# First loads in another order with zeros multiplied meanwhile, VectorE in written order around the latents' norm, and the gates' running sum moved behind six attention steps

## The chip, the cores and the metric

The kernel runs on one core of a Trainium2 chip. The metric is the device time of one execution in microseconds (us); lower is better. Everything below is about the start of a program whose profiled span is 3190.3 us, and about the same place in its second layer. "TensorE" is the engine of the matrix products (PE in the profile; its weight loads are PEld), "VectorE" is DVE, "ScalarE" is ACT, "GpSimd" is POOL, "SyncE" is SP, and the last one only issues loads and stores here.

## The reference

Two blocks of two layers each run one behind the other on 512 tokens of width 1024, all in fp32. The change touches the first block alone. Each of its layers begins with one product of the tokens with a wide weight matrix, whose columns are cut into the inputs of four kinds of attention:

```python
def first_block(x, w_in, fox_b_f, mla_g_q, mla_g_kv, mla_w_uq, mla_w_ukv, swa_sinks, mix_g, w_o, ...):
    for l in range(DEPTH):
        h = x @ w_in[l]
        (fq, fk, fv, fgate, cq, ckv, kr, sq, sk, sv, wq, wk, wv) = jnp.split(h, points, axis=-1)
        log_f = jax.nn.log_sigmoid(fgate + fox_b_f[l])
        cum = jnp.cumsum(log_f, axis=1).transpose(0, 2, 1)
        out_a = _causal_softmax_blocks(_heads(fq, FOX_H), _heads(fk, FOX_H), _heads(fv, FOX_H),
                                       HEAD_DIM ** -0.5, cum)
        out_b = _mla(cq, ckv, kr, mla_g_q[l], mla_g_kv[l], mla_w_uq[l], mla_w_ukv[l], cos, sin)
        out_c = _stick_breaking_blocks(_heads(sq, SB_H), _heads(sk, SB_H), _heads(sv, SB_H))
        out_d = _swa_sink_alibi(_heads(wq, SWA_H), _heads(wk, SWA_KV_H), _heads(wv, SWA_KV_H),
                                swa_sinks[l], slopes)
        ...  # mix, output product, layer norm, feed-forward network, layer norm

def _mla(cq, ckv, kr, g_q, g_kv, w_uq, w_ukv, cos, sin):
    q = (_rmsnorm(cq, g_q) @ w_uq).reshape(B, S, MLA_H, MLA_NOPE + MLA_ROPE)
    kv = (_rmsnorm(ckv, g_kv) @ w_ukv).reshape(B, S, MLA_H, MLA_NOPE + MLA_V)
    ...
```

Three pieces matter here. The *latents* are `cq` (256 columns), `ckv` (128) and the rope key `kr` (32); `cq` and `ckv` are normed and then multiplied with `mla_w_uq` and `mla_w_ukv`. The four columns `fgate` are the gates, whose running sum of logarithms `cum` enters the scores of `out_a` alone (called fox in the kernel). `wq`, `wk` and `wv` feed `out_d`.

## The kernel before

**Products.** An fp32 product is made of three products of high and low parts: high weight by high x, high weight by low x, low weight by high x (`mm3`, lines 157 to 161; the last of the three is line 160). The high part is a cast on ScalarE, the low part a subtraction on VectorE. For x these tiles are XH and XL, for weights `whi` and `wlo`. `wchunk` (line 138) loads a chunk of weights into one of three `raw` buffers from SyncE's queue; unless the caller does it himself (`split=False`), it makes `whi` (line 145) and `wlo` (line 148), of which there are four buffers each. A later load into a raw buffer waits until the cast and the subtractions that read it are done.

**What sets the order.** TensorE's instructions stand in the order in which the code is written. On the other engines a scheduler puts the instructions in order by its own costs, except inside a `tc.manual_schedule` of that engine: there too the written order holds. At the start of the first layer this is so for VectorE and ScalarE, up to `order.close()`. An engine takes its instructions strictly in the order of the program that comes out, so an instruction that waits holds up all that stand behind it. `later(t, f)` puts the products of f into TensorE's order after t us of further products, by the code's own cost of a product.

**The start of a layer.** In layer 0, x arrives in four blocks of 128 tokens (`load_x`), and `turn_x` transposes two blocks at a time on TensorE (tile xT); ScalarE copies the result to XH, VectorE makes XL, and ScalarE copies it once more to X. In layer 1 XH and XL come out of the layer norm before. Then comes *hg*: the product of the 420 columns 768 to 1188 of `w_in` (gates, cq, ckv, kr), loaded as two chunks of four row blocks with 260 columns and two with 160, with some of the columns written twice in another order. `half_units` makes hg for one half of the tokens after the other, 96 products of 256 columns each; in layer 0 the transposes of the second half of x stand among those of the first. ScalarE copies the latents out to `lat`, VectorE the rope key and the gates to `mz` (line 738).

Behind hg stand, in written order: `tables` (rope, masks, sel and alibi tables, loaded from GpSimd's queue and cast on VectorE), `lat_norm` (sum of squares `s`, and by `later` their sums on TensorE, the inverse root in 12 small VectorE instructions, its broadcast on TensorE, and the high and low parts LH and LL of the normed latents), `forget` (the rotated key `rope`, and the gates' running sum: Identity, Abs, Exp and Ln on ScalarE, a scan on VectorE, written to CR), `g_mla_w` (the weights `mla_w_uq` and `mla_w_ukv` are loaded and split into `uhl` and `kvhl`), and two *units* of 512 tokens by 256 weight columns each (`g_unit` at column 1956 for wq, at 2212 for wk and wv; tile u). A unit takes two chunks of four row blocks, so 16 steps of three products of 512 columns. The call `flush()` puts what `later` still holds ahead of the rest. The products that use LH and LL (`drain(gw)`) come after the first unit and half of the second.

**The attention steps.** Then 64 steps run in a pipeline with a lag of three (`run_steps`): scores into one of two PSUM banks (sc), exponential on ScalarE (PR), transpose (pt, copied to PT), product with the values (pv). The pauses are filled with the products of further units. Steps 0 to 15 are `_mla`, 16 to 31 `out_d`, 32 to 47 stick breaking, and 48 to 63 fox, the only ones that read CR.

## Time and profile before

| what | value |
|---|---|
| runs | 3192.87, 3191.55, 3190.7 us (median 3191.55 us) |
| profiled execution | 3192.1 us, of which its span is 3190.3 us |
| mean granted TensorE clock | 0.998 |
| busy, TensorE | 3150.4 us (99% of the span) |
| busy, VectorE | 1611.0 us (50%) |
| busy, ScalarE | 1164.5 us (37%) |
| busy, GpSimd | 128.3 us (4%) |
| moved by DMA | 289.95 MB, mean 91 GB/s |

The span is the time between the first and the last instruction of the profiled execution; its own time has 1.8 us more around it. A busy TensorE is not one at its peak: when the granted clock is at half, its products take longer and it counts as busy all the same.

### The profile page before, as it was taken

Reading aid. Unit: us, or ns where it says so; the run is one execution under the profiler, and the core shown is the slowest. Engines: PE = TensorE matmul, PEld = TensorE weight load, DVE = VectorE, ACT = ScalarE, POOL = GpSimd, SP = SyncE. Lnnn points to the kernel's source line nnn. Section 1 sums busy time; section 2 is a strip of 40 time slices with the busy share of each in tenths; the row PEclk is TensorE's granted clock in tenths of the full one; section 3 lists DMA queues with packets and bytes.
Section 4 is the critical chain, followed back from the end, with each engine's and each line's share of the span. In section 5 each row is a group of like instructions: output and inputs, shape, how many; then the busy total and the mean of one; then the engine's idle time right before and its main releaser. Section 6 shows DMA issues by size and latency. Waiting matters only on the chain.

```text
span 3190.3 us, 40511 instructions
## 1 busy us (share of the span) xinstructions
PE 3150.4 (99%) x16376; PEld 2657.1 (83%) x16376; DVE 1611.0 (50%) x2804; ACT 1164.5 (37%) x1945; POOL 128.3 (4%) x176
## 2 busy tenths in 40 slices
PE   8999999999999999999999999999999999999999
PEld 7878888997788888988888788888888888788888
DVE  6566333475664334844336764433444336754433
ACT  5454322264533222533224443322323224443322
POOL 1002000020020000000001000000000000000000
PEclk9999999999999999999999999999999999999999
DMA  4111333341113333333333223333333333133322
GB/s 140 47 40 54 111 99 96 109 133 40 54 54 100 99 96 116 114 95 99 95 97 95 81 80 93 99 96 96 95 103 93 96 106 89 57 95 101 96 95 84
DMA packets 285355, 289.95 MB, mean 91 GB/s; under 512 B 10260, under 2 KB 282208, under 8 KB 285168
## 3 DMA queue, kind: packets, MB, share of 16 engines
q1 hardware_dynamic: 281792, 281.15, 29.4%
q0 software_dynamic: 2944, 5.17, 0.6%
q8 instruction: 128, 2.10, 0.3%
q10 hardware_dynamic: 432, 1.05, 0.1%
q14 instruction: 59, 0.48, 0.0%
HBM read 285.22 MB, written 2.11 MB: 90 GB/s over the span
## 4 chain that ended last, share of the span: by engine, by line
PE 94%; DVE 4%; ACT 1%; issue 1%; DMA 0%; DVEq 0%; SPq 0%; ACTq 0%
PE u L158 17%; PE u L160 17%; PE u L159 17%; PE o L159 7%; PE o L158 7%; PE o L160 7%; PE pv L638 2%; PE oh L158 2%; PE oh L159 2%; PE oh L160 2%; PE pt L631 1%; PE hg L158 1%; PE hg L159 1%; PE hg L160 1%; PE sc L951 1%; PE ut L520 1%
## 5 line engine op out<-in xcount | busy, mean ns | idle before, releaser
L148 DVE TENSOR_TENSOR wlo<-raw,whi 128x1024 fp32r<-128x1024 f32 (+2 forms) x570 | 651.8, 1146 | 847.4 <-ACT whi L145 845.8
L158 PE MATMUL u<-XH,whi 128*128 128x512 f32 x2496 | 979.7, 393 | 0.0
L160 PE MATMUL u<-XH,wlo 128*128 128x512 f32 x2496 | 972.3, 390 | 0.0
L159 PE MATMUL u<-XL,whi 128*128 128x512 f32 x2496 | 971.7, 389 | 0.0
L145 ACT CAST whi<-raw 128x1024 fp32r<-128x1024 f32 (+1 forms) x534 | 549.1, 1029 | 961.8 <-PE o L159 421.4
L160 PEld LDWEIGHTS u<-XH,wlo 128*128 128x128 f32 x2496 | 468.5, 188 | 98.4
L158 PEld LDWEIGHTS u<-XH,whi 128*128 128x128 f32 x2496 | 469.0, 188 | 97.3 <-issue 2.2
L159 PEld LDWEIGHTS u<-XL,whi 128*128 128x128 f32 x2496 | 468.9, 188 | 94.5
L158 PE MATMUL o<-hh,whi 128*128 128x512 f32 x836 | 325.6, 389 | 0.0
L160 PE MATMUL o<-hh,wlo 128*128 128x512 f32 x836 | 325.3, 389 | 0.0
L159 PE MATMUL o<-hl,whi 128*128 128x512 f32 x836 | 325.2, 389 | 0.0
L571 ACT ACTIVATE gs<-gs 128x512 f32<-128x512 f32 x88 | 55.5, 632 | 407.2 <-DVE gs L569 407.0
L159 PEld LDWEIGHTS o<-hl,whi 128*128 128x128 f32 x836 | 156.9, 188 | 32.5
L160 PEld LDWEIGHTS o<-hh,wlo 128*128 128x128 f32 x836 | 156.9, 188 | 32.5
L158 PEld LDWEIGHTS o<-hh,whi 128*128 128x128 f32 x836 | 156.9, 188 | 32.5
L570 DVE TENSOR_TENSOR us<-u,SA 128x512 f32<-128x512 f32 x86 | 59.5, 692 | 165.2 <-PE u L160 165.2
L158 PE MATMUL oh<-hh,whi 128*128 128x256 f32 x440 | 125.0, 284 | 0.0
L159 PE MATMUL oh<-hl,whi 128*128 128x256 f32 x440 | 124.5, 283 | 0.0
L160 PE MATMUL oh<-hh,wlo 128*128 128x256 f32 x440 | 124.5, 283 | 0.0
L569 DVE TENSOR_TENSOR gs<-u,SA 128x512 f32<-128x512 f32 x86 | 59.0, 686 | 89.2 <-PE u L160 89.2
L159 PE MATMUL hg<-XL,whi 128*128 128x256 f32 x320 | 94.3, 295 | 3.5 <-POOL XL L408 3.2
L158 PE MATMUL hg<-XH,whi 128*128 128x256 f32 x320 | 94.6, 296 | 2.1 <-ACT whi L710 2.1
(393 smaller groups left out, 3876.8 us busy)
## 6 DMA issues: line engine op xcount, KB each, us to landing
raw<-ffn_gate SPq DMA_DIRECT2D x88, 512.0 KB, 3.8
raw<-ffn_up SPq DMA_DIRECT2D x88, 512.0 KB, 3.7
raw<-ffn_down SPq DMA_DIRECT2D x82, 512.0 KB, 3.4
raw<-w_in SPq DMA_DIRECT2D x76, 512.0 KB, 3.7
raw<-w_down SPq DMA_DIRECT2D x54, 512.0 KB, 3.5
raw<-w_gate SPq DMA_DIRECT2D x44, 512.0 KB, 3.8
raw<-w_up SPq DMA_DIRECT2D x44, 512.0 KB, 3.8
raw<-w_o SPq DMA_DIRECT2D x16, 512.0 KB, 3.5
```

The lines of the kernel that those rows point to most:

```text
L145: SC.copy(hv, rv)
L148: V.tensor_sub(lv[:, ks], rv[:, ks], hv[:, ks].bitcast(F32))
L158: T.matmul(ps, wh, xh, start=start, stop=False)
L159: T.matmul(ps, wh, xl, start=False, stop=False)
L160: T.matmul(ps, wl, xh, start=False, stop=stop)
L520: T.matmul(ps, XH[:, k, js], wh[:, k % 4], start=(k == 0), stop=False)
L569: V.tensor_mul(v(gs), v(g), bcv)
L570: V.tensor_mul(v(us), v(u), bcv)
L571: SC.activation(gs, gs, AF.Silu)
L631: T.transpose(pt[:, a * P:(a + 1) * P], self.pr[:, a * P:(a + 1) * P], ident)
L638: T.matmul(self.pv_out(), self.pts[:, a * P:(a + 1) * P], self.vfn(j), start=(a == 0), stop=(a == len(self.kb) - 1))
L951: T.matmul(pr["s"][b_][:, :nk], *ops(b_), start=True, stop=False)
```

## The change

It has three parts.

- *The start of layer 0.* While the first loads run, TensorE multiplies zeros: 11 products of bf16 tiles that nothing reads (`wake`). The third block of x is loaded from ScalarE's queue instead of SyncE's. In both layers the 420 columns are loaded in four chunks of two row blocks (128 x 2 x 420, 430 KB) instead of two pairs of four row blocks, with the casts and subtractions of each; a `whi` and a `wlo` tile now take two chunks. ScalarE's copies to X move from behind the XH casts to behind the casts of the third chunk, and for the second half of x to behind the last XH cast (a `copies` of their own). The rope, sel and alibi tables are loaded from SyncE's queue instead of GpSimd's.
- *VectorE in written order.* From `lat_norm` to the `flush()` behind the first eight steps of unit 2212, VectorE's instructions stand in written order (`calm`), in both layers.
- *The gates' running sum.* `forget` keeps the rope part; the rest becomes `forget_sum`, which is called when step 6 of the attention steps is issued, in both layers.

```diff
--- before
+++ after
@@ -208,7 +208,15 @@
 
 
     def load_x(xin, j):
-        (nc.scalar if j == 0 else nc.sync).dma_start(xin[j], A["x"][0, j * P:(j + 1) * P, :])
+        (nc.scalar if j in (0, 2) else nc.sync).dma_start(xin[j], A["x"][0, j * P:(j + 1) * P, :])
+
+    def wake():
+
+        z = tp.tile([P, 512], BF16, tag="tmp", bufs=6, name="zeros")
+        V.memset(z, 0.0)
+        ps = pvt("wake")
+        for i in range(11):
+            T.matmul(ps, z[:, :P], z, start=True, stop=True)
 
     def turn_x(xin, hh):
         hs = slice(hh * HALF, (hh + 1) * HALF)
@@ -221,15 +229,19 @@
                                 xin[2 * hh + b][:, (t + m) * P:(t + m + 1) * P], ident)
             xps.append((t, ps))
 
-        def parts(n):
+        def parts(n, keep=True):
 
             for t, ps in xps[parts.done:parts.done + n]:
                 SC.copy(XH[:, t:t + 2, hs], ps)
                 V.tensor_sub(XL[:, t:t + 2, hs], ps, XH[:, t:t + 2, hs].bitcast(F32))
             parts.done += n
-            if parts.done == len(xps):
-                for t, ps in xps:
-                    SC.copy(X[:, t:t + 2, hs], ps)
+            if parts.done == len(xps) and not keep:
+                parts.copies()
+
+        def copies():
+            for t, ps in xps:
+                SC.copy(X[:, t:t + 2, hs], ps)
+        parts.copies = copies
         parts.done = 0
         return parts
 
@@ -674,15 +686,15 @@
             G.dma_start(sink, A["swa_sinks"][l].partition_broadcast(P))
 
             def tables():
-                G.dma_start(rope, A["c_rope"])
+                nc.sync.dma_start(rope, A["c_rope"])
                 if l == 0:
                     load_columns()
                     load_masks(ap_)
                 sr = tmp("sr")
-                G.dma_start(sr.rearrange("p (h k) -> p h k", h=4), A["c_sel"])
+                nc.sync.dma_start(sr.rearrange("p (h k) -> p h k", h=4), A["c_sel"])
                 ar = [tmp("ar"), tmp("ar")]
                 for hh in range(2):
-                    G.dma_start(ar[hh].rearrange("p (h k) -> p h k", h=2), A["c_alibi"][:, 2 * hh:2 * hh + 2])
+                    nc.sync.dma_start(ar[hh].rearrange("p (h k) -> p h k", h=2), A["c_alibi"][:, 2 * hh:2 * hh + 2])
                 V.tensor_mul(fb, fb, fe)
                 V.tensor_reduce(bf, fb, axis=AX.X, op=ALU.add)
                 V.tensor_scalar(nsink, sink, -1.0, None, op0=ALU.mult)
@@ -697,37 +709,45 @@
                 order.enter_context(tc.manual_schedule(engines={mybir.EngineType.DVE, mybir.EngineType.Activation}))
                 load_x(xin, 0)
                 load_x(xin, 1)
+                wake()
             chq, chm = [], []
-            for k0 in (0, 4):
-                rf = wchunk(w_in, k0 * P, 4, 768, 260, split=False)
-                rk = wchunk(w_in, k0 * P, 4, 1028, 160, split=False)
-                if l == 0 and k0 == 0:
+            if l == 0:
+                splits = turn_x(xin, 0)
+
+            def gate(ap):
+                return ap[:, :, 192:256].rearrange("p k (r h) -> p k r h", h=4)
+            cut = ((slice(0, 160), slice(260, 420)), (slice(160, 176), slice(404, 420)),
+                   (slice(176, 192), slice(388, 404)))
+            for k0 in range(0, ND, 2):
+                rf = wchunk(w_in, k0 * P, 2, 768, 420, split=False)
+                if l == 0 and k0 == 2:
                     load_x(xin, 2)
+                if l == 0 and k0 == 4:
                     load_x(xin, 3)
-                    splits = turn_x(xin, 0)
-                    splits(1)
-                hi, lo = wsplit(4, 256)
+                if l == 0 and k0 < 4:
+                    splits(2)
+                if k0 % 4 == 0:
+                    chq.append(wsplit(4, 256))
+                    chm.append(wsplit(4, 256))
+                ks = slice(k0 % 4, k0 % 4 + 2)
+                hi, lo = [t[:, ks] for t in chq[-1]]
                 SC.copy(hi, rf[:, :, 4:260])
                 V.tensor_sub(lo, rf[:, :, 4:260], hi.bitcast(F32))
-                chq.append((hi, lo))
-                hi, lo = wsplit(4, 256)
-
-                def gate(ap):
-                    return ap[:, :, 192:256].rearrange("p k (r h) -> p k r h", h=4)
-                gsrc = rf[:, :, 0:4].unsqueeze(2).to_broadcast([P, 4, 16, 4])
-                parts = ((slice(0, 160), slice(0, 160)), (slice(160, 176), slice(144, 160)),
-                         (slice(176, 192), slice(128, 144)))
-                for dst, src in parts:
-                    SC.copy(hi[:, :, dst], rk[:, :, src])
+                hi, lo = [t[:, ks] for t in chm[-1]]
+                gsrc = rf[:, :, 0:4].unsqueeze(2).to_broadcast([P, 2, 16, 4])
+                for dst, src in cut:
+                    SC.copy(hi[:, :, dst], rf[:, :, src])
                 SC.copy(gate(hi), gsrc)
-                for dst, src in parts:
-                    V.tensor_sub(lo[:, :, dst], rk[:, :, src], hi[:, :, dst].bitcast(F32))
+                for dst, src in cut:
+                    V.tensor_sub(lo[:, :, dst], rf[:, :, src], hi[:, :, dst].bitcast(F32))
                 V.tensor_sub(gate(lo), gsrc, gate(hi).bitcast(F32))
-                chm.append((hi, lo))
-                if l == 0 and k0 == 0:
-                    splits(3)
+                if l == 0 and k0 == 4:
+                    splits.copies()
             if l == 0:
-                later(4.0, lambda: turn_x(xin, 1)(4))
+                def second_half():
+                    splits = turn_x(xin, 1)
+                    splits(4, False)
+                later(4.0, second_half)
             lat = [ap_.tile([P, 544], F32, tag=tg, name="lat")[:, :S] for tg in ("om", "cp", "wv")]
             mz = tmp("mz")
             res = half_units([chq, chm])
@@ -770,6 +790,8 @@
                     later(5.2, lambda: bc((2,), 0))
                     later(5.9, lambda: bc((0, 1), NB))
                 later(5.5, stats)
+            calm = ExitStack()
+            calm.enter_context(tc.manual_schedule(engines={mybir.EngineType.DVE}))
             lat_norm()
 
 
@@ -781,6 +803,8 @@
                 V.tensor_mul(rope[0:32], mz[0:32], rope[0:32])
                 V.tensor_mul(rt1[0:32], mz[32:64], rope[32:64])
                 V.tensor_add(rope[0:32], rope[0:32], rt1[0:32])
+
+            def forget_sum():
 
                 e, one = tmp("e"), tmp("one")
                 hp = slice(64, 128)
@@ -1093,6 +1117,7 @@
             for _ in range(8):
                 next(wkv)
             flush()
+            calm.close()
             drain(gw)
             drain(g_mla_qk(0))
             for _ in range(4):
@@ -1111,6 +1136,7 @@
             def more(q, ks, start):
                 return lambda: fill.gens.append(g_wo(q, ks, start, False))
             LAG = 3
+            on(6, forget_sum)
             on(16 + LAG + 1, lambda: norm_group(1))
             on(32 + LAG + 1, lambda: norm_group(3))
             on(48 + LAG + 1, lambda: fill.need(10), flush, lambda: turn_group(1, 0), lambda: norm_group(2))
@@ -1574,7 +1600,7 @@
             for j in range(NB):
                 load_x(xin, j)
             for hh in range(2):
-                turn_x(xin, hh)(4)
+                turn_x(xin, hh)(4, False)
         flush()
     for l in range(n1):
         layer1(l)
```

TensorE's own order is the same in both kernels but for the 11 products of zeros. Three places show how the others' move.

VectorE in layer 0, around the first unit u. The names: `uhl` and `kvhl` are low parts of the latents' weights, `mz<-hg` copies gates and rope key out of hg, `wlo<-raw,whi` are the low parts of u's chunks. Before:

```order
L841 TENSOR_TENSOR uhl<-raw,uhl 128x8x96
L841 TENSOR_TENSOR uhl<-raw,uhl 128x8x16 x2
L171 TENSOR_TENSOR kvhl<-raw,kvhl 128x512
L738 COPY mz<-hg 128x256
L148 TENSOR_TENSOR wlo<-raw,whi 128x1024 x3
L738 COPY mz<-hg 128x256
```

So two rows of `uhl`, one of `kvhl` and three of `wlo` stood ahead of the copy of the second half of hg. In the changed kernel both mz copies (`L758 COPY mz<-hg 128x256 x2`) come first, then six small rows for masks, gates and sinks, and then:

```order
L701 CAST sel<-sr 128x512
L703 CAST alibi<-ar 128x512 x2
L818 CAST CR<-sel 64x512
L771 TENSOR_TENSOR s_506<-s_506,s_507 128x512
L803 TENSOR_TENSOR rope<-mz,rope 32x512
L804 TENSOR_TENSOR rt_515<-mz,rope 32x512
L698 TENSOR_TENSOR fb<-fb,fe 128x4
L805 TENSOR_TENSOR rope<-rope,rt_515 32x512
L865 TENSOR_TENSOR uhl<-raw,uhl 128x8x96
L865 TENSOR_TENSOR uhl<-raw,uhl 128x8x16 x2
L171 TENSOR_TENSOR kvhl<-raw,kvhl 128x512
L148 TENSOR_TENSOR wlo<-raw,whi 128x1024 x2
```

The low parts of the latents' weights and of u's chunks have moved behind the second copy of mz, the tables' casts, the squares' sum and the rope. The order in layer 1 is alike, without the masks and with the tables' casts ahead of the second mz copy.

SyncE's queue of loads from the start of the program to the units' first chunks; O is the buffer in which a block of x arrives, `raw<-w_in` with 260, 160 or 420 columns are hg's chunks and with 256 those of the units. Before:

```order
L136 DMA ident<-c_ident 128x128
L211 DMA O_99<-x 128x1024
L141 DMA raw<-w_in 128x4x260
L141 DMA raw<-w_in 128x4x160
L211 DMA O_100<-x 128x1024
L211 DMA O_101<-x 128x1024
L141 DMA raw<-w_in 128x4x260
L141 DMA raw<-w_in 128x4x160
L141 DMA raw<-mla_w_uq 128x2x384
L141 DMA raw<-mla_w_ukv 128x512
L141 DMA raw<-w_in 128x4x256 x16
```

In the changed kernel:

```order
L136 DMA ident<-c_ident 128x128
L211 DMA O_99<-x 128x1024
L141 DMA raw<-w_in 128x2x420 x3
L211 DMA O_101<-x 128x1024
L689 DMA rope<-c_rope 128x512
L141 DMA raw<-w_in 128x2x420
L141 DMA raw<-mla_w_uq 128x2x384
L141 DMA raw<-mla_w_ukv 128x512
L141 DMA raw<-w_in 128x4x256
L694 DMA sr<-c_sel 128x512
L697 DMA ar<-c_alibi 128x512 x2
L141 DMA raw<-w_in 128x4x256 x15
```

Three of hg's smaller chunks now stand ahead of the fourth block of x, the third block has gone to ScalarE's queue, and the tables stand among the weights' loads.

ScalarE and the gates' running sum in layer 0; `e` and `mz` are its tiles, PR the exponentials of the steps, QH and KH the heads' queries and keys. Before, it stood behind the squares of the latents:

```order
L787 ACTIVATE mz<-mz,bf 64x512
L750 ACTIVATE s_471<-lat 128x512
L788 ACTIVATE e<-mz 64x512
L789 ACTIVATE e<-e 64x512
L790 ACT_TABLE_LOAD
L790 ACTIVATE e<-e 64x512
L886 ACTIVATE wqk<-u 128x512
L877 COPY KH<-rope 32x512
```

In the changed kernel it stands among the steps' exponentials:

```order
L893 ACTIVATE QH<-uq 64x512
L632 COPY PT<-pt 128x384
L812 ACTIVATE e<-mz 64x512
L813 ACTIVATE e<-e 64x512
L814 ACT_TABLE_LOAD
L814 ACTIVATE e<-e 64x512
L1001 ACT_TABLE_LOAD
L1001 ACTIVATE PR,rs<-sc,nm 128x256
L632 COPY PT<-pt 128x128
```

Its three functions and two table loads now lie between the copy of a transpose and the exponential of the step behind it; the first function (the biased `mz`) has stayed where it was.

## Rows read from the trace of the kernel before

**Rows 1.** Part 1 of the profile's page: busy time, share, instructions of each engine.

```profile
PE 3150.4 (99%) x16376; PEld 2657.1 (83%) x16376; DVE 1611.0 (50%) x2804; ACT 1164.5 (37%) x1945; POOL 128.3 (4%) x176
```

**Rows 2.** Timeline of TensorE, 0 to 41 us: start, duration, instructions, idle time before.

```profile
6.09 3.46 PE L220 MATMUL xT<-ident,O 128*128 128x128 f32 x15 [0.77 <-DMA O<-x]
11.66 0.58 PE L158 MATMUL hg<-XH,whi 128*128 128x256 f32 x1 [2.11 <-ACT whi L710]
...
13.30 0.42 PE L158 MATMUL hg<-XH,whi 128*128 128x256 f32 x1
...
18.64 0.30 PE L159 MATMUL hg<-XL,whi 128*128 128x256 f32 x1
...
19.96 1.91 PE L220 MATMUL xT<-ident,O 128*128 128x128 f32 x16
21.63 0.36 PE L158 MATMUL hg<-XH,whi 128*128 128x256 f32 x1
...
40.06 0.40 PE L158 MATMUL u<-XH,whi 128*128 128x512 f32 x1
```

**Rows 3.** Window 300:302 of TensorE: us, busy us (instructions), granted clock, DMA share, GB/s.

```profile
300.00:302.00 2.00, 2.00 (x11) 0.50 0.02 5
```

**Rows 4.** Chain of waits, 0 to 120 us: start, duration, work.

```profile
1.66 8.88 DMA raw<-w_in
```

**Rows 5.** Timeline of TensorE around the norms' sums.

```profile
57.42 0.84 PE L195 MATMUL sc<-ident,ry 128*128 128x128 f32 x6 [2.83 <-DVE p L1190]
...
298.73 1.02 PE L283 MATMUL st<-cst,SQ 128*128 128x1 f32 x4 [3.04 <-DVE SQ L379]
...
305.30 0.32 PE L160 MATMUL hg<-XH,wlo 128*128 128x256 f32 x1
...
946.46 0.61 PE L283 MATMUL st<-cst,SQ 128*128 128x1 f32 x4 [3.04 <-DVE SQ L379]
...
950.35 0.36 PE L159 MATMUL hg<-XL,whi 128*128 128x256 f32 x1
```

**Rows 6.** Waits of TensorE, 660 to 730 us.

```profile
PE sc L1038 <- DVE QH L873: 0.2, 1, 0.2
```

**Rows 7.** DMA queues, 6 to 9 us: packets, MB, share of 16 engines.

```profile
q1 hardware_dynamic: 505, 0.52, 55.5%
q0 software_dynamic: 105, 0.12, 40.7%
```

**Rows 8.** Timeline of VectorE, 34 to 50 us.

```profile
34.79 2.36 DVE L148 TENSOR_TENSOR wlo<-raw,whi 128x1024 fp32r<-128x1024 f32 x2 [5.22 <-ACT whi L145]
...
41.69 0.42 DVE L738 COPY mz<-hg 128x256 f32<-128x256 f32 x1
...
42.49 0.67 DVE L781 TENSOR_TENSOR rope<-mz,rope 32x512 f32<-32x512 f32 x1
...
44.35 0.68 DVE L782 TENSOR_TENSOR rt<-mz,rope 32x512 f32<-32x512 f32 x1
45.06 0.69 DVE L751 TENSOR_TENSOR s<-s,s 128x512 f32<-128x512 f32 x1
...
48.73 0.42 DVE L794 CAST CR<-sel 64x512 fp32r<-64x512 f32 x1
```

**Rows 9.** Timeline of ScalarE, 38 to 90 us.

```profile
41.21 0.65 ACT L748 ACTIVATE s<-lat 128x512 f32<-128x512 f32 x1
...
46.05 1.28 ACT L790 ACT_TABLE_LOAD   x1
...
83.46 0.47 ACT L977 ACTIVATE PR<-sc,nm 128x256 f32<-128x256 f32 x1 [2.22 <-DVE nm L973]
```

**Rows 10.** Timeline of VectorE in layer 1.

```profile
670.97 1.35 DVE L841 TENSOR_TENSOR uhl<-raw,uhl 128x768 fp32r<-128x768 f32 x3
672.24 0.68 DVE L171 TENSOR_TENSOR kvhl<-raw,kvhl 128x512 fp32r<-128x512 f32 x1
```

**Rows 11.** DMA issues, 0 to 60 us: count, KB each, median us to landing.

```profile
raw<-w_in SPq DMA_DIRECT2D x9, 512.0 KB, 3.7
```

## The prediction

> **What bounds the kernel now.** I read the busy shares first [rows 1]: TensorE is busy for 3150.4 us of 3190.3 us, so a change pays only where TensorE stands idle or runs slowly, and it costs wherever it makes TensorE wait. Next I read TensorE's timeline at the start [rows 2]. The 16 transposes of the first half of x are done near 9.55 us, the first product of the latents (tile hg) starts at 11.66 us, and the 25 products from 13.30 to 18.64 us follow each other at 0.2136 us, while the 153 from 21.63 to 40.06 us follow at 0.1205 us. The slow pace is that of the half clock: where the windows print a granted clock of 0.50 (1.2 GHz instead of 2.4) [rows 3], the same form runs at it too. The printed clock of the first 20 us is 1.00, so there I go by the pace. The chain of waits says why hg starts late [rows 4]: the load of the first weight chunk ends at 10.54 us.
>
> After hg (call F the start of the unit u that follows, 40.06 us in layer 0) TensorE works on without a pause up to one wait of 2.83 us for the latents' norm, at 54.6 to 57.42 us in layer 0 [rows 5]. Layer 1 has nothing of the kind: from 660 to 730 us TensorE waited 0.2 us in all [rows 6]. So the whole change works on about 6.5 us: some 3.6 us of the start and 2.83 us in layer 0.
>
> **The start (first loads, zeros).** From 11.66 to 40.06 us TensorE took 28.4 us for 192 hg products and 16 transposes [rows 2]. At the fast pace that is 192 x 0.1205 + 1.67 (19.96 to 21.63) = 24.8 us. In the changed kernel the 11 products of zeros need only a memset and keep TensorE busy from about 1.3 to 6 us (11 x 0.427, my estimate as twice the slow 256-column pace), the transposes follow, and the clock may rise before hg. In the rows, work after a pause ran 3.9 us (946.46 to 950.35) to 6.6 us (298.73 to 305.30) at the half clock [rows 5], so it should be up at 5 to 8 us. When does the first chunk land? It is now 430 KB (two row blocks of 420 columns) behind the second block of x, which came at 6.09 us. From 6 to 9 us the SP queue had 55.5% of the DMA engines' time and POOL's 40.7%, with 0.52 and 0.12 MB [rows 7]; a 256 KB table of POOL's queue now goes to SP, behind the fourth block of x. At those 0.64 MB in 3 us the chunk takes 2.0 us and lands at 8.1 us; at the old chunk's 532 KB in 4.45 us it takes 3.6 us and lands at 9.7 us; at worst it lands at 10.5 us as now. I take 8.9 us, the middle of the first two. A cast of 512 columns later (0.65 us) hg starts, at 9.55 us. On the way new waits arise, about 2.5 us by the written order: the low parts of the first chunk are five subtractions on VectorE (1.1 us beyond what TensorE can use), and the second half's transposes wait for PSUM banks that the X copies free, and those copies now stand behind the casts of the third chunk on ScalarE (1.1 us, and 0.3 us elsewhere). F = 9.55 + 24.8 + 2.5 = 36.85 us: **3.2 us gained**. Bounds: landing at 8.1 us and 1.5 us of waits gain 5.0 us; landing at 10.5 us and a clock still at half (25 x 0.093 = 2.3 us) lose 0.7 us.
>
> **VectorE in written order, layer 0.** Before, the low parts (wlo) of u's two weight chunks were made at 34.79 to 37.15 us [rows 8], between the two copies of mz and so ahead of F. Now the order says that VectorE reaches them behind the second mz copy, which reads the last hg product. The stream between is strictly behind F: ScalarE's lat copy ends at F + 0.6. From mz to the end of the two alibi casts the rows take 44.35 - 41.69 = 2.66 us, less 0.67 us for the rope product that stood among them: 2.0 us. CR takes 0.42 us: F + 3.0. The sum s waits for ScalarE: three lat copies, two squares, the biased mz and the third square, 0.8 + 1.06 + 0.75 + 0.65 us with rows of 0.65 us for 512 columns [rows 9], so F + 3.45; s takes 0.65 us, the three rope steps 2.1 us: F + 6.2. Then come the low parts of uhl, 1.3 us, kvhl 0.6 us [rows 10], and u's first wlo, 1.2 us (half of the pair's 2.36): **F + 9.3**. TensorE uses two of its three products of the first step (0.48 us) and waits 8.8 us for the third.
>
> One more load is late: u's second chunk goes into the raw buffer that uhl's subtraction frees at F + 7.5. It lands 3.7 us later [rows 11], its cast takes 1.05 us and its wlo 1.22 us: F + 13.5. A step of three 512-column products takes about 0.72 us (6 x 0.1205), so at the full clock TensorE would be there at F + 12.2 and wait 1.3 us. But a pause of 3.04 us dropped the clock twice, one of 2.83 us did not [rows 3, 5]; one of 8.8 us will, I take it. At half clock four steps take 5 us and the second wait is covered; the clock itself costs 0.436 of the slow stretch (1 - 0.1205/0.2136), with 3.9 to 6.6 us 1.7 to 2.9 us; I take 2.3 us.
>
> The 2.83 us wait goes: the norm's inverse root stands at about F + 22, TensorE comes to its broadcast at about F + 26. Behind it, in written order, the low parts of two later chunks stand ahead of those of the latents, the last of them waiting for a load whose buffer is freed only at about F + 23.6; TensorE needs the latents' low parts about 0.9 us before they are there (0 to 1.5). Layer 0: 8.8 + 2.3 + 0.9 - 2.8 = **9.2 us lost** (7.3, with no clock drop but the second wait, to 10.4).
>
> **Layer 1.** The same order without masks, small tables and the alibi casts behind F (they stand ahead of the second mz copy): mz at F + 1.5, s at F + 3.5, rope F + 5.6, uhl 6.85, kvhl 7.45, wlo F + 8.7: 8.2 us of waiting, 2.3 us of clock, 0.9 us at the latents, and no old wait to set against it: **11.4 us lost** (9.5 to 12.6).
>
> **The running sum behind six steps.** Its ScalarE block (three functions of 0.63 us, two table loads of 1.28 us) is 4.45 us in one piece ahead of the exponential of step 5, before which ScalarE idles for 2.22 us today [rows 9]. So that exponential comes 2.2 us later, and TensorE's scores of step 7 need its bank. At that stage TensorE has little other work to fill in. Both layers: **4.4 us lost** (2 if half is caught up, 7 if VectorE's scan comes on top).
>
> Splitting hg's chunks in four costs ten more small instructions on each of two engines; in layer 1 they lie under the last products of the layer before.
>
> **Sum.** -3.2 + 9.2 + 11.4 + 4.4 = +21.8 us on the profiled run's 3192.1 us. That run stands 0.55 us above the median of 3191.55 us: **3213 us**.
>
> **Rivals.**
> 1. The start gains nothing. For it: VectorE and ScalarE get more and smaller work there, and the chunk's landing is unknown. Landing at 10.5 us costs 1.6 us more (3215 us), with the clock at half besides 3.9 us (3217 us). The Trainium skill, DMA: Bandwidth & Descriptors, section "Issuing engines are not separate DMA queues", says that the issuing engine changes only the issue time since all queues run on the same 16 engines; the 55.5% and 40.7% of one stretch [rows 7] agree that they share. By that page moving loads between queues gives nothing, and this rival's 3215 us would be the time.
> 2. The running sum is hidden: the steps have a lag of three, and TensorE's fill could cover 2 us a layer. Against it, the scores have two banks only. 3209 us.
> 3. The clock does not fall in the long waits, or rises at once; the second wait returns. About 1 us less in each layer: 3211 us.
> 4. Faster: u's low parts are there in time after all, since VectorE had time before F. Then nothing waits at u, the 2.83 us are saved, and with the sum hidden: 3192.1 - 3.2 - 2.8 = 3186 us. It decides when the two waits together fall below about 6 us. Against it: VectorE can't pass the second mz copy, and the rows behind that copy alone are 8 us and more.
> 5. No change: waits of some 3 us a layer against the start's gain. Nothing in the rows shortens VectorE's list to a third.
>
> **How the numbers follow.** The forecast as worked out gets 0.60; rival 1 0.13, rival 2 0.13, rival 3 0.08, rival 4 0.03, rival 5 0.03. All bounds together give 13.8 to 30.7 us more (3205 to 3222 us); both ends need all terms at one side, so 8 in 10 lie in 3204 to 3220 us, one us under the low bound for what the list may overstate. A measurement here can tell some 0.2% (6.4 us) from no change: faster 0.03, same 0.04, slower 0.93.
>
> **What would show it.** In the changed trace: hg at the fast pace from about 9.5 us on, F near 37 us; TensorE idle for 8 to 9 us with its first u step, waiting for wlo, in both layers, and a granted clock of 0.5 behind; no wait at the norm's broadcast; two table loads inside the steps with TensorE waiting 2 us. I am wrong if VectorE makes u's wlo before F, or if the second raw chunk is long there.

## The result: 3216.69 us, 0.8% slower

The changed kernel takes 3216.69 us (median of 4 runs, 3216.28 to 3217.46) where the kernel before takes 3191.45 us (4 runs, 3190.7 to 3192.87); the ratio is 1.0079, with a 95% interval of 1.0066 to 1.0092. The profiled execution took 3216.58 us with a span of 3214.8 us at a mean granted clock of 0.993. The page's busy line of the changed kernel:

```profile
PE 3160.9 (98%) x16387; PEld 2661.1 (83%) x16387; DVE 1615.3 (50%) x2825; ACT 1166.1 (36%) x1965; POOL 124.4 (4%) x168
```

TensorE's busy time rose by 10.5 us against [rows 1]: 4.0 us of it are the 11 products of zeros, the rest is longer time for the same products. TensorE works through the same order in both kernels, so the time at which it starts one and the same product tells what each stretch cost (F is the start of the first unit u, as in the prediction):

| TensorE starts | before, us | after, us | after minus before | stretch | predicted |
|---|---|---|---|---|---|
| first hg product | 11.66 | 9.00 | -2.66 | | |
| first unit u, layer 0 (F) | 40.06 | 35.48 | -4.58 | start: -4.6 | -3.2 |
| scores of step 0 | 69.18 | 73.25 | +4.07 | unit and norm: +8.65 | +9.2 |
| third scores of 512 columns (step 11) | 92.92 | 102.14 | +9.22 | running sum: +5.15 | +2.2 |
| first unit u, layer 1 | 690.64 | 699.15 | +8.51 | layer in between: -0.7 | 0 |
| scores of step 0, layer 1 | 716.49 | 735.49 | +19.00 | unit: +10.5 | +11.4 |
| third scores of 512 columns | 740.57 | 764.36 | +23.79 | running sum: +4.8 | +2.2 |
| end of the span | 3190.3 | 3214.8 | +24.5 | rest: +0.7 | 0 |

TensorE's timeline of the changed kernel has the places (start, duration, instructions, idle time before and what ended it):

```profile
1.28 4.04 PE L219 MATMUL wake<-zeros 128*128 128x512 bf16 x11 [1.28 <-DVE zeros L216]
...
6.11 1.86 PE L228 MATMUL xT<-ident,O 128*128 128x128 f32 x15 [0.67 <-DMA O<-x]
9.00 0.39 PE L158 MATMUL hg<-XH,whi 128*128 128x256 f32 x1 [1.04 <-ACT whi L734]
...
9.95 0.28 PE L158 MATMUL hg<-XH,whi 128*128 128x256 f32 x1
...
15.36 1.94 PE L228 MATMUL xT<-ident,O 128*128 128x128 f32 x16 [0.94 <-DMA O<-x]
...
35.48 0.40 PE L158 MATMUL u<-XH,whi 128*128 128x512 f32 x1
35.72 0.40 PE L159 MATMUL u<-XL,whi 128*128 128x512 f32 x1
44.92 0.79 PE L160 MATMUL u<-XH,wlo 128*128 128x512 f32 x1 [8.80 <-DVE wlo L148]
...
60.66 1.03 PE L195 MATMUL sc<-ident,ry 128*128 128x128 f32 x8
...
88.15 0.33 PE L643 MATMUL pt<-ident,PR 128*128 128x128 f32 x1 [0.65 <-DVE PT L634]
90.49 2.08 PE L1062 MATMUL sc<-KH,QH 96*128 96x512 f32 x2 [2.01 <-ACT PR L1001]
...
102.14 1.02 PE L1062 MATMUL sc<-KH,QH 96*128 96x512 f32 x2
...
707.21 0.80 PE L160 MATMUL u<-XH,wlo 128*128 128x512 f32 x1 [7.43 <-DVE wlo L148]
...
752.73 2.07 PE L1062 MATMUL sc<-KH,QH 96*128 96x512 f32 x2 [1.93 <-ACT PR L1001]
```

The reader is to see four things. The zeros run from 1.28 to 5.32 us and the transposes take 1.86 us where they took 3.46 us [rows 2]; hg starts at 9.00 us and has the fast pace from 9.95 us on. The first unit's third product waits 8.80 us in layer 0 and 7.43 us in layer 1, and takes 0.8 us there, where the product ahead of it took 0.40 us. The norm's broadcast at 60.66 us waits for nothing, where it waited 2.83 us before [rows 5]. And a new wait stands ahead of the scores of step 7, 2.01 us in layer 0 and (at 752.73 us) 1.93 us in layer 1; these scores take 2.08 us, those of step 11 at 102.14 us, of the same form, 1.02 us.

The chain of waits of the changed kernel (start, duration, work) has the first chunk's load, which ended at 10.54 us before [rows 4], and the load of the third block of x:

```profile
1.65 6.66 DMA raw<-w_in
...
8.34 6.88 DMA O<-x
```

The chunk is there at 8.31 us. The third block is issued only at 8.34 us, since its load now stands in ScalarE's queue behind ScalarE's first casts, and the transposes of the second half (15.36 us) wait for it.

VectorE's timeline of the changed kernel shows why the first unit waits, in the order that the change wrote:

```profile
36.09 0.42 DVE L758 COPY mz<-hg 128x256 f32<-128x256 f32 x1 [11.09 <-ACT lat L757]
...
39.08 0.69 DVE L771 TENSOR_TENSOR s<-s,s 128x512 f32<-128x512 f32 x1 [0.49 <-ACT s L770]
39.69 0.67 DVE L803 TENSOR_TENSOR rope<-mz,rope 32x512 f32<-32x512 f32 x1
...
41.18 0.67 DVE L805 TENSOR_TENSOR rope<-rope,rt 32x512 f32<-32x512 f32 x1
41.78 1.34 DVE L865 TENSOR_TENSOR uhl<-raw,uhl 128x768 fp32r<-128x768 f32 x3
43.06 0.67 DVE L171 TENSOR_TENSOR kvhl<-raw,kvhl 128x512 fp32r<-128x512 f32 x1
43.66 1.21 DVE L148 TENSOR_TENSOR wlo<-raw,whi 128x1024 fp32r<-128x1024 f32 x1
48.07 1.23 DVE L148 TENSOR_TENSOR wlo<-raw,whi 128x1024 fp32r<-128x1024 f32 x1 [3.21 <-ACT whi L145]
```

The second mz copy comes 0.6 us behind F, the squares' sum at F + 3.6, the rope until F + 6.4, uhl, kvhl, and u's first low part ends at 44.87 us, F + 9.4. The second chunk's low part comes at 48.07 us, behind a cast that waited for the load. The granted clock (windows: us, busy us and instructions, clock, DMA share, GB/s) is at half behind both kinds of wait:

```profile
40.00:44.00 4.00, 0.00 (x0) 0.50 0.01 0
...
46.00:48.00 2.00, 2.00 (x6) 0.50 1.07 365
...
88.00:90.00 2.00, 0.33 (x1) 0.92 0.00 0
...
92.00:94.00 2.00, 2.00 (x10) 0.50 0.00 0
```

ScalarE's timeline around the second has the running sum's last function between two table loads, and the exponential that the scores of step 7 wait for only behind them:

```profile
86.64 1.28 ACT L814 ACT_TABLE_LOAD   x1
87.93 0.63 ACT L814 ACTIVATE e<-e 64x512 f32<-64x512 f32 x1
88.58 1.28 ACT L1001 ACT_TABLE_LOAD   x1
89.87 0.47 ACT L1001 ACTIVATE PR<-sc,nm 128x256 f32<-128x256 f32 x1
```

### The profile page after: what moved, and what is told of

Its sections match the earlier page's. It is cut to its first block, busy times and chain, and to the rows that moved or that the text cites. A ratio compares the mean times of both kernels' runs of the same rounds, so it can differ in the third digit from the quotient of the medians.

```text
span 3214.8 us, 40560 instructions
## 1 busy us (share of the span) xinstructions
PE 3160.9 (98%) x16387; PEld 2661.1 (83%) x16387; DVE 1615.3 (50%) x2825; ACT 1166.1 (36%) x1965; POOL 124.4 (4%) x168
## 3 DMA queue, kind: packets, MB, share of 16 engines
q1 hardware_dynamic: 280752, 282.73, 29.3%
q8 instruction: 129, 2.11, 0.3%
HBM read 285.22 MB, written 2.11 MB: 89 GB/s over the span
## 4 chain that ended last, share of the span: by engine, by line
PE 93%; DVE 4%; ACT 2%; DMA 1%; issue 1%; SPq 0%; DVEq 0%; ACTq 0%
PE u L158 17%; PE u L160 17%; PE u L159 17%; PE o L158 7%; PE o L159 7%; PE o L160 7%; PE pv L650 2%; PE oh L158 2%; PE oh L159 2%; PE oh L160 2%; PE pt L643 1%; PE sc L975 1%; DVE wlo L148 1%; PE hg L158 1%; PE ut L532 1%; PE hg L159 1%
```

## The experiments

Twelve kernels were run, each with a profile. The numbers below are medians of device time; the stretches are cut as in the table above, all from the profiled executions, in us:

| kernel | median, us | start to F | F to step 0 | steps 0 to 11 | between | layer 1: F to step 0 | steps 0 to 11 | rest |
|---|---|---|---|---|---|---|---|---|
| before | 3191.45 | 40.1 | 29.1 | 23.7 | 597.7 | 25.9 | 24.1 | 2449.7 |
| after | 3216.69 | 35.5 | 37.8 | 28.9 | 597.0 | 36.3 | 28.9 | 2450.4 |
| e1_no_calm | 3192.15 | 35.4 | 26.1 | 28.8 | 598.3 | 25.8 | 29.2 | 2449.2 |
| e2_calm_only | 3223.98 | 38.5 | 42.8 | 23.7 | 596.3 | 46.4 | 24.5 | 2451.2 |
| e3_sum_only | 3197.47 | 39.5 | 26.1 | 29.0 | 596.3 | 25.9 | 29.2 | 2449.7 |
| e4_start_only | 3188.79 | 35.6 | 30.7 | 23.8 | 596.9 | 25.9 | 24.1 | 2450.1 |
| e5_no_wake | 3218.44 | 35.2 | 39.0 | 29.1 | 597.0 | 37.6 | 29.5 | 2450.2 |
| e6_pool_tables | 3215.88 | 35.5 | 38.6 | 29.0 | 596.9 | 36.4 | 29.0 | 2449.7 |
| e7_products_in_wait | 3211.80 | 35.2 | 38.4 | 26.0 | 598.7 | 37.0 | 26.0 | 2448.9 |
| e8_sum_before_steps | 3209.38 | 35.1 | 39.4 | 23.7 | 597.1 | 37.4 | 24.1 | 2451.0 |
| e9_u_first | 3196.36 | 35.1 | 28.2 | 29.3 | 597.1 | 26.9 | 29.5 | 2450.2 |
| e10_u_first_sum_early | 3191.71 | 35.2 | 29.4 | 23.7 | 597.0 | 28.9 | 24.0 | 2450.4 |
| e11_sum_before_step0 | 3193.31 | 35.4 | 26.1 | 28.1 | 598.0 | 25.8 | 27.2 | 2450.3 |
| e12_products_at_u | 3215.85 | 35.2 | 38.5 | 29.2 | 597.0 | 36.3 | 29.2 | 2448.9 |

Where TensorE meets neither a wait nor a fall of the clock, a stretch comes out within 0.1 us in one kernel after the other (steps of 23.7 and 24.1 us, a unit of 25.8 or 25.9 us); with the long waits the same code varies by up to 1.3 us (37.8 to 39.0, 36.3 to 37.6), and the columns "between" and "rest" by 1 to 2 us. The theory: VectorE's written order makes the waits at the first unit, ScalarE's table loads make the wait in the steps, each with a fall of the clock behind it. The rivals: the loads' new order or chunks, the tables' queue, or knock-on delays.

**The changed kernel without VectorE's written order.**

```diff
-            calm = ExitStack()
-            calm.enter_context(tc.manual_schedule(engines={mybir.EngineType.DVE}))
...
-            calm.close()
```

> The changed kernel without VectorE's written order: the scheduler puts the low parts of the first unit's chunks ahead of the second mz copy again, as before the change; the rest of the change stays. Theory (the written order makes the two waits of 8.8 us at the first unit, worth 8.65 us in layer 0 and 10.5 us in layer 1 by the two traces): no wait at the first unit in either layer, the 2.8 us wait at the latents' norm may come back in part; the start keeps its 4.6 us, the running sum its 9.9 us of loss: 3194 to 3198 us. Rival (the waits come from the chunks' new loads or from the tables on SyncE's queue, and the written order only lays them there): still over 3205 us, with TensorE waiting at the first unit or at its second chunk.

It took 3192.15 us (3191.66 to 3195.12), ratio to before 1.0003 (0.9993 to 1.0012), 2 us under the range. TensorE waits nowhere at the first unit, and VectorE's timeline has the two low parts at 30.08 us, ahead of F, as before the change:

```profile
30.08 2.36 DVE L148 TENSOR_TENSOR wlo<-raw,whi 128x1024 fp32r<-128x1024 f32 x2 [5.22 <-ACT whi L145]
...
36.97 0.42 DVE L758 COPY mz<-hg 128x256 f32<-128x256 f32 x1
```

The norm's broadcast does not wait either (TensorE's longest wait from F to step 0 is 0.2 us), so that stretch is 3.0 us shorter than before the change: what held up the norm before was the running sum among VectorE's instructions, not the scheduler's order as such. The theory holds; the written order alone is worth the 11.7 and 10.5 us of the two stretches.

**The kernel before with the written order alone**, and **with the moved running sum alone** (the edits of the change, one at a time).

> The kernel before with VectorE's written order alone; the gates' running sum is then in one piece ahead of the low parts too. Theory: mz, tables, s, rope, then the sum's min, scan and CR (some 3.5 us more, since they wait for ScalarE's two table loads), then uhl, kvhl and the first low part: TensorE waits 11 to 13 us at the first unit in both layers, and the norm's 2.8 us wait goes: 3191.5 + 11 to 13 + 13 to 15 = 3215 to 3220 us. Rival (the written order costs only together with the new start): 3191 to 3195 us.

> The kernel before with the gates' running sum behind six steps alone. Theory (ScalarE's three functions and two table loads stand ahead of an exponential whose bank the scores of step 7 need; a wait of some 2 us and a fall of the clock behind it, 5 us in each layer): 3191.5 + 10 less up to 2.8 us if the norm's wait goes with the scan: 3198 to 3202 us, with the clock at half near the step in both layers. Rival (the sum is hidden in the steps unless the steps come late): 3189 to 3192 us.

The first took 3223.98 us (ratio 1.0102, 1.0087 to 1.0117), 4 us above the range; the second 3197.47 us (1.0018, 1.0009 to 1.0027), half a microsecond under its range. In the first, VectorE's timeline has u's low part only behind the scan, since the whole running sum stands in its order:

```profile
45.39 0.69 DVE L793 SCALAR_TENSOR_TENSOR e<-mz,e 64x512 f32<-64x512 f32 x1 [0.47 <-ACT e L792]
...
46.65 1.22 DVE L795 TENSOR_TENSOR_SCAN mz<-one,e 64x512 f32<-64x512 f32 x1
...
51.14 1.22 DVE L148 TENSOR_TENSOR wlo<-raw,whi 128x1024 fp32r<-128x1024 f32 x1
```

TensorE's waits in it (engine, line, releaser: us in total, times, longest), from 0 to 140 and from 680 to 790 us:

```profile
PE u L160 <- DVE wlo L148: 13.2, 1, 13.2
...
PE u L160 <- DVE wlo L148: 14.6, 1, 14.6
```

In layer 1 the stretch lost 20.5 us, 5.9 us more than this wait. The granted clock was at half for 17 us there, but TensorE worked only in the last 5.2 us of them; it was at half once more for 3.4 us (0.58 and 0.57 in the windows from 742 to 746 us), behind waits of 0.96 and 0.28 us. An estimate with the prediction's share of 0.436 for a slow stretch gives 3.7 us for the two falls and 1.2 us for the two waits, 5 of the 5.9 us; the expectation had counted neither. In the second kernel the norm's wait is gone (stretch of 26.1 us, as in the first experiment) and each layer's steps lose 5.2 us. So each of the two parts costs by itself, and the rivals (that the written order needs the new start, that the sum is hidden unless the steps come late) have fallen.

**The start alone** (no written order; `forget_sum()` called right behind `forget()`).

> The start alone: loads in the new order, four chunks, zeros multiplied, the copies to X later, tables from SyncE's queue; VectorE ordered by the scheduler, the running sum in its old place. Theory (the start gains 4.6 us and costs nothing elsewhere): 3186 to 3188 us, with TensorE's first unit at 35.5 us. Rival (the four chunks' smaller pieces or the tables among the weights' loads cost in layer 1 or at the norm what the start gains): 3190 us or more.

3188.79 us (3188.26 to 3190.28), ratio 0.9992 (0.9983 to 1.0001): 2.9 us less than the 3191.69 us of the kernel before beside it, at the edge of what can be told. F is 4.4 us earlier, layer 1 costs nothing, but 1.6 us are given back at the norm: its wait is as long as before, and this time the clock falls behind it. TensorE's timeline:

```profile
52.99 1.06 PE L195 MATMUL sc<-ident,ry 128*128 128x128 f32 x8 [2.85 <-DVE p L1213]
...
54.35 0.63 PE L160 MATMUL u<-XH,wlo 128*128 128x512 f32 x1
```

and its window behind the broadcast:

```profile
54.00:56.00 2.00, 2.00 (x7) 0.58 0.53 179
```

In the kernel before, the window behind the same wait (57.42 us [rows 5]) has the full clock:

```profile
58.00:60.00 2.00, 2.00 (x13) 1.00 0.75 234
```

**Without the zeros**, and **with the tables on GpSimd's queue** (the call of `wake()` left out; `G.dma_start` for rope, sel and alibi again).

> The changed kernel without the 11 products of zeros. Theory (the zeros raise the clock before the first product): the transposes run at the half clock as before, hg starts 0.5 to 1 us later and runs at the slow pace of 0.2136 us to about 17 or 18 us: 3 to 5 us lost, 3219.5 to 3222 us. Rival (the start's gain is all in the loads, the first chunk being there sooner): hg at the slow pace but the loads' and the splits' own waits hide it: 3216 to 3218 us.

> The changed kernel with the rope, sel and alibi tables loaded from GpSimd's queue again. Theory (the queue of a small load does not matter here, since the queues share the engines and the tables are not needed early): 3216 to 3218 us, hg starting within 0.5 us of 9.0 us. Rival (the rope table's 256 KB on GpSimd's queue takes the DMA engines from the first chunk, as they shared them between 6 and 9 us before the change): hg starts 0.6 to 1.6 us later, 3217.3 to 3218.5 us.

Both took the changed kernel's time: 3218.44 us (3215.32 to 3219.66) and 3215.88 us (3214.95 to 3218.26). F is at 35.20 and 35.51 us. For the tables that is what the theory said. For the zeros the time lies between the rival's range and the theory's and decides nothing, but the theory's mechanism fell, as TensorE's timeline without them shows:

```profile
5.99 3.46 PE L228 MATMUL xT<-ident,O 128*128 128x128 f32 x15 [0.75 <-DMA O<-x]
9.10 0.56 PE L158 MATMUL hg<-XH,whi 128*128 128x256 f32 x1
...
10.08 0.28 PE L158 MATMUL hg<-XH,whi 128*128 128x256 f32 x1
```

The transposes run slowly again (3.46 us), but they end where the first chunk lands, TensorE goes on with hg at 9.10 us without a pause, and the fast pace is there from 10.08 us. In the kernel before, hg came 2.11 us behind the transposes and the fast pace only at 18.64 us [rows 2]. So, by elimination, the start's gain is the loads': 2.66 us at hg itself, since its first chunk lands at 8.31 instead of 10.54 us, and 1.9 us behind it, where the fast pace comes at about 10 us. The zeros shorten transposes that nobody waits for. Of the loads, order, chunk size and the third block's queue were not run apart, nor were the later copies to X.

**Products that nobody reads in the wait of step 7**: eight of 512 columns, ahead of its scores.

```diff
+            def spare7():
+                ps = mmt("spare")
+                for _ in range(8):
+                    T.matmul(ps, XH[:, 0, :P], XH[:, 1], start=True, stop=True)
+                return make7()
```

> The changed kernel with eight more products of 512 columns that nothing reads, just ahead of the scores of step 7, where TensorE waits 2 us behind the running sum; nothing else moves. Theory (of the 5.0 us that the sum costs in each layer some 2 us are the wait and some 3 us the clock, which falls to half there): the products fill the wait, the clock stays up, and each layer gets back 2.5 to 3 us: 3210.5 to 3212 us. Rival (the 3 us beside the wait are knock-on delays of the steps behind, not the clock): 3216 to 3218 us.

3211.80 us (3210.94 to 3212.25). The table loads still hold the exponential up to the same point, but the clock does not fall, and each layer's steps take 26.0 us instead of 28.9. TensorE's timeline:

```profile
88.60 2.07 PE L1161 MATMUL spare<-XH 128*128 128x512 f32 x8
90.87 1.13 PE L1062 MATMUL sc<-KH,QH 96*128 96x512 f32 x2 [0.20 <-ACT PR L1001]
```

and the window that was at half in the changed kernel:

```profile
92.00:94.00 2.00, 2.00 (x17) 1.00 0.04 8
```

So of the 5 us that the running sum costs in a layer, 2.3 us (layer 1: 1.9 us) are the wait (26.0 against 23.7 and 24.1) and 2.9 us the clock (28.9 against 26.0).

**The running sum ahead of the steps**, outside the written order.

```diff
             calm.close()
+            forget_sum()
             drain(gw)
...
-            on(6, forget_sum)
```

> The changed kernel with the gates' running sum called ahead of the products with the normed latents, outside VectorE's written order, instead of behind six steps. Theory (the sum costs nothing where ScalarE idles, and VectorE's part of it falls into the time in which the first unit's second low part waits for its load): the sum's loss of 5.15 and 4.8 us goes: 3206 to 3208 us. Rival (its two table loads and the scan push the second low part or the latents' high parts later): 3209 to 3214 us.

3209.38 us (3209.01 to 3209.74): the steps are as short as before the change, but the unit is 1.7 and 1.1 us longer than in the changed kernel, of which 0.6 and 0.7 us are the first wait (9.38 and 8.08 us): the scheduler put a memset of the sum ahead of u's first low part. It put the scan between the two low parts, so that the second starts 1.3 us later behind F. The rest is within the scatter of this stretch. That is the rival's outcome; the sum was not free on VectorE there.

**The first unit's chunks ahead of the mz copies**, with the sum in the steps and then with the sum early.

```diff
             res = half_units([chq, chm])
+            ch_u = [wchunk(w_in, k0 * P, 4, 1956, 256) for k0 in (0, 4)]
...
-            drain(g_unit(w_in, 1956, wq_evac))
+            drain(g_chunks(ch_u, wq_evac))
```

> The changed kernel with the first unit's two chunks loaded and split right behind hg's products in the code, ahead of the mz copies, so that VectorE's written order has their two low parts first; all else stays in written order. Theory (the place of the two low parts in VectorE's order is the whole cost of the written order): no wait at the first unit in either layer; both blocks' 8.65 and 10.5 us come back, and the norm's old wait of 2.8 us in layer 0 stays away: 3193.5 to 3198 us. Rival (behind them the latents' weights and the next unit's chunks are then late instead): waits at the second unit or at the latents' products, 3200 us or more.

> As the run with the first unit's chunks ahead, and the gates' running sum called ahead of the products with the normed latents. Theory (start 4.6 us and norm 2 to 2.8 us gained, nothing lost): 3184 to 3187.5 us, faster than both kernels by more than the start alone. Rival (the sum's scan and table loads in front of the norm's small instructions bring the old norm wait back): 3187 to 3191 us.

The first took 3196.36 us (3194.64 to 3197.99): VectorE's order is still the written one, only the two low parts stand first in it, and the waits at the unit are gone; behind it TensorE waits 0.6 and 0.3 us for the latents' parts LH and LL. It is the sharpest test of the theory, and the theory holds. The two loads move ahead too, but in the changed kernel the first low part waited for no load, only for the rows ahead of it. VectorE's timeline:

```profile
29.80 2.36 DVE L148 TENSOR_TENSOR wlo<-raw,whi 128x1024 fp32r<-128x1024 f32 x2 [8.60 <-ACT whi L145]
...
35.68 0.42 DVE L759 COPY mz<-hg 128x256 f32<-128x256 f32 x1 [3.18 <-ACT lat L758]
```

The second took 3191.71 us (3190.51 to 3193.34), ratio 1.0000 (0.9991 to 1.0010), outside both expectations: now low parts of the second unit come late behind the scan, and the two stretches from F to step 0 are 3.3 and 3.1 us longer than 26.1 and 25.8 us. TensorE's timeline:

```profile
50.67 0.50 PE L160 MATMUL u<-XH,wlo 128*128 128x512 f32 x1 [1.89 <-DVE wlo L148]
```

**The new start, scheduled VectorE, the sum ahead of step 0** (`forget_sum()` behind `drain(g_mla_qk(0))`).

> The new start with VectorE ordered by the scheduler, and the gates' running sum called behind the first head's queries and keys, ahead of step 0, so that ScalarE's functions and table loads stand ahead of the exponential of step 0, whose bank is not needed before the scores of step 2. Theory (the sum costs where it stands ahead of an exponential that TensorE waits for, and it caused the norm's wait where it stood ahead of the inverse root): no norm wait, no wait at step 7, no more than 0.5 us at step 2: 3183.5 to 3187 us, faster than the start alone (3188.8 us). Rival (ScalarE's 4.5 us are late for TensorE at any place in the steps): TensorE waits 2 us near step 2 or 3 with the clock at half behind it, 3189 to 3195 us.

3193.31 us (3190.19 to 3194.70), in the rival's range. The norm's wait is gone, but the exponential of step 1 then waits for VectorE's maximum, which stands behind the scan, and the scores of step 3 for that exponential. ScalarE's timeline:

```profile
70.39 0.47 ACT L999 ACTIVATE PR<-sc,nm 128x256 f32<-128x256 f32 x1 [1.35 <-DVE nm L995]
```

and TensorE's:

```profile
71.00 1.12 PE L1060 MATMUL sc<-KH,QH 96*128 96x512 f32 x2 [2.70 <-ACT PR L999]
```

Behind it the clock falls in layer 0 (0.61 and 0.53 from 72 to 76 us). In layer 1 the same wait is 2.27 us and the clock stays at 1.00.

**Products that nobody reads in the wait at the first unit**: 30 between the second and the third product.

> The changed kernel with 30 more products of 512 columns that nothing reads between the second and the third product of the first unit's first step, where TensorE waits 8.8 and 7.4 us; nothing else moves. Theory (behind the long wait the half clock costs about 1.7 us, and while it lasts it hides that the second chunk is late): the clock stays up, the wait for the second chunk's low part comes in its place, 1 to 2 us in each layer, and the time changes by less than 2 us: 3214.5 to 3217 us. Rival (the second chunk is there in time, and the clock's part comes back in full in both layers): no second wait, 3212.5 to 3214 us.

3215.85 us (3214.31 to 3217.60), as the theory said. The clock stays at full speed, what is left of the first wait is 2.01 us, and the second chunk is then waited for (0.52 us listed in layer 0, 0.62 and 0.53 us in layer 1). The profile counts a wait only from the modelled end of the product ahead; by the starts of u's products, against the run without the written order, this second wait costs 1.5 and 1.8 us, and the half clock cost 1.8 us in both layers of the changed kernel. So the one took what the other gave back. TensorE's timeline:

```profile
35.63 6.97 PE L165 MATMUL spare<-XH,whi 128*128 128x512 f32 x30
44.61 0.50 PE L167 MATMUL u<-XH,wlo 128*128 128x512 f32 x1 [2.01 <-DVE wlo L148]
...
48.95 0.50 PE L167 MATMUL u<-XH,wlo 128*128 128x512 f32 x1 [0.52 <-DVE wlo L148]
```

No version beats both kernels beyond doubt: the start alone is 2.9 us ahead of the kernel before, with an interval that ends at 1.0001. A kernel with the stretches of 35.4, 26.1, 23.7, 25.9 and 24.1 us together would stand some 8 us under the kernel before, but every place that was tried for the running sum costs a part of that again, and whether a better one exists stays open.

## Why the prediction was right, step by step

The forecast was 3213 us in 3204 to 3220 us, with 0.93 for slower; it came out at 3216.69 us, and by the mechanism that was named.

- *First unit, layer 0.* Forecast: low part at F + 9.3, a wait of 8.8 us, net 9.2 us lost. Measured: F + 9.4, 8.80 us, 8.65 us lost. The list of VectorE's rows in the new order was the whole calculation; one sum in it is off, since the four ScalarE terms ahead of s make 3.26 us and not the 3.45 us used (s began at F + 3.6). By the starts of the products, against the run without the written order, 1.8 us went to the half clock behind the wait, where the text had 2.3 us. The second wait was rightly put under the half clock: the run with extra products there, which is rival 3's condition, brought it back, and the time moved by 0.8 us, within the runs' scatter, where rival 3 was given 1 us a layer.
- *First unit, layer 1.* Forecast 11.4 us with a wait of 8.2 us; measured 10.5 us and 7.43 us. Most of the difference is that s was done at F + 3.0 us instead of F + 3.5 us; the rows behind it took 5.0 us instead of 5.2 us.
- *Norm.* The 2.83 us wait went, as forecast. The wait for LL is listed at 0.28 us, but by the starts of the products around it 0.8 us were lost there, where the text had 0.9 us. One part of the reason was incomplete: the wait went also where the scheduler kept VectorE's order and only the scan was moved.
- *Start.* Forecast 3.2 us, measured 4.6 us. hg came at 9.0 instead of 9.55 us, and from there to F 1.7 us were lost instead of 2.5 us: 0.22 us in a wait for a low part, 0.94 us in one for the third block of x, none for the X copies, and the rest in no listed wait. The text had not seen that the third block's move to ScalarE's queue makes it late (15.22 us, above). What it put down to the zeros was the loads' doing. The 4.6 us are measured against an F of 40.06 us in one profile; two other kernels with the old start had 39.53 and 38.54 us, so a gain of 3.1 to 4.6 us is as much as can be said.
- *Running sum.* The one mis-sized term: "Both layers: 4.4 us lost" was 9.9 us. The wait was as worked out (2.01 and 1.93 us against 2.2), but the fall of the clock, which the text counted behind the long waits, was left out behind this short one, 2.9 us a layer. This excess of 5.5 us outweighs the 2.8 us by which the other terms were too high; that the total came within 4 us is in part luck, since the two errors offset each other. The Trainium skill, ScalarE: Activation LUTs, section "Table sets: the hidden batching unit", has a set that holds both Exp and Ln, so that the two would need no switch between them; the rows here have a load of 1.28 us on either side of the one Ln, so this kernel does not use it, and no run tried it.
- *Rivals.* Rival 1 (no gain at the start) fell: F came 4.6 us sooner. The Trainium skill, DMA: Bandwidth & Descriptors, section "Issuing engines are not separate DMA queues", agrees with the run that gave the tables back to GpSimd's queue (F 35.51 against 35.48 us): the tables' queue gave nothing. What gave the gain is by elimination the order and size of the other loads. Rival 2 (the sum hidden) fell. Rivals 4 and 5 would have needed waits of 6 or 3 us; VectorE could not pass the mz copy.

## What to carry to other kernels

Before an engine is put into written order, list what stands ahead of the first thing that the bottleneck waits for, with each row's duration and what it waits for itself; here that sum was right to 0.1 us in layer 0 and to 0.8 us in layer 1. Allow for the clock at every pause of a busy TensorE: in the steps a 2 us wait cost 5 us, though not every wait of that length did. Where a whole change loses, run its parts singly, since here the start alone was 2.9 us ahead, at the edge of what can be told, while the other parts lost 28 us on top of it.

## What the runs showed of the hardware that was not expected

- A pause's length does not tell whether the clock falls. At the norm a wait of 2.83 us left it up in the kernel before [rows 5], one of 2.85 us at the same place dropped it to half in the start-only kernel, and in the steps a wait of 2.01 us dropped it, with one of 0.65 us just ahead (TensorE was busy for 0.33 us of the 2 us from 88 us on). Waits of 0.96 and 0.28 us close together dropped it in the written-order-only kernel, and one of 2.27 us ahead of step 3 in layer 1 of the run with the sum ahead of step 0 did not.
- The full clock came within 4.1 us of the transposes' start (5.99 to 10.08 us) where TensorE went on without a pause, at half speed all the while, and 12.6 us after it (6.09 to 18.64 us) where a pause of 2.11 us stood in between. In two other kernels with the old start, the written-order-only and the sum-only one, the fast pace came at 15.33 and 17.52 us, so F of the kernel before is itself uncertain by some 1.5 us (40.06, 39.53 and 38.54 us in three profiles).
